# Moving a gate's sum to another stage, column groups for modulation sums, row halves for retention scores, and a shorter Newton step

## The chip, the cores and the metric

The kernel runs on one core of a Trainium2 chip. The metric is the device time of one execution of the program in microseconds (us). The engines are TensorE (PE), VectorE (DVE), ScalarE (ACT), GpSimd (POOL) and SyncE (SP); each runs its own list of instructions in order and waits on semaphores for the others. DMA transfers are issued from SP's, ACT's and POOL's lists.

## What is computed

One layer of a diffusion backbone over 1024 latent tokens (x) and 256 context tokens, 1024 wide, in fp32:

```python
mod = silu(c) @ w_ada + b_ada            # 1 x 6144
sh_a, sc_a, gt_a, sh_f, sc_f, gt_f = split(mod, 6)
h = rms_norm(x, g_attn) * (1 + sc_a) + sh_a      # context: the same with c_ctx
rq, rk, rv, rg, cq, ckv, kpe = split(h @ w_in)
y_ret = bidirectional chunkwise retention (4 heads, chunks of 128), group norm, swish gate
y_mla = multi-head latent attention (4 heads), keys from context and latent tokens
x_mid = x + gt_a * (concat(y_ret, y_mla) @ w_out)
h2 = rms_norm(x_mid, g_ffn) * (1 + sc_f) + sh_f
x = x_mid + gt_f * (square(relu(h2 @ w_ff1)) @ w_ff2)
out = rms_norm(x, g_final)
```

## The kernel before

Every product of fp32 operands is made as three matmuls on halves (`mm3`, L96 to L100): `split` (L102 to L104) makes a high half by an ACT cast and a low half by a DVE subtraction. The stages follow one another: modulations of the attention part, input projection, retention, attention, output projection, up stage and down stage of the MLP, final norm. A scheduler turns the program's order into one list for each engine. Large tiles live in 45 SBUF slots that are handed out first in, first out (`Slots`, L35 to L50), so a load can be issued when the slot's former user is done; small ones are in a ring of six (`tmp`); PSUM has eight banks, handed out in rings.

*Modulations.* gt_a, sh_f, sc_f and gt_f are the groups g=2, 3, 4 and 5 of 1024 columns of w_ada. For each, eight slices of w_ada (128 rows each, 512 KB) are loaded by SP (`mod_load`, L430; the load itself L160), and DVE adds them up, scaled by silu(c) of their row (`mod_step`, L435 to L450: L442 for the first, L444 for seven more). What is left is a sum over 128 partitions, made by PE with a matrix of ones (`mod_fin`, L455 to L473). Gates 2 and 5 are wanted as a row (L462): b_ada is added on one partition, the row goes to `g_dram`, and is loaded from there into all partitions. g=4 and g=3 are wanted as columns `mcol` (L471). The first modulations of the kernel, sh_a and sc_a, have their own code (L275 to L284): their matmuls with 32 columns of weights go to four 32-column groups, and a copy (L281) and transposes (L284) follow. g=2, 4 and 3 are summed in the input projection, g=5 in the output projection.

*Retention scores.* In `ret_a2` (L586 to L599) each chunk has four score matmuls (L597), two for each half of the 128 rows of `qkT`: heads g=0 on rows 0 to 63, g=1 on rows 64 to 127. Each half has its own bank, and two masks (`tt`) evacuate them.

*Newton step.* `rstd_of` (L106 to L119) makes 1/sqrt(v) by Ln and Exp on ACT and one Newton step on DVE, for each row of a tile. w is the number of values of a row; w=1 except for the group norm of retention.

*Output projection* (loop at L1323). 14 steps `wseq` over halves hf of the columns and token tiles t follow two that are issued earlier. At its start the four quarters of w_out's second half are loaded (L958), multiplied by gate gt_a (L959) and split. In the first eight steps two slices of g=5 are added and two loaded; the sum is finished at n == 9. `h2` is then normalised (L1354) and transposed (L245).

*Up stage* (loop over `order`, 112 steps). The product h2 @ w_ff1 is made by a Strassen-Winograd scheme: for each of 16 column pairs p there are seven products q of 12 matmuls. DVE and ACT prepare weights four steps ahead, evacuate the banks, and apply the squared ReLU; SP loads w_ff1 and stores the results (L1164).

Of the kernel before, what the change touches and what calls it, by code (L numbers as in the profile page):

```python
# [12 lines left out]
F32 = mybir.dt.float32  # L13
F32R = mybir.dt.float32r
AF = mybir.ActivationFunctionType
ALU = mybir.AluOpType
AX = mybir.AxisListType

P = 128
D = 1024  # L20
KD = D // P
# [7 lines left out]
EPS = 1e-6  # L29
# [24 lines left out]
def hymba_block(ctx: ExitStack, tc: tile.TileContext, A, K, out):  # L54
    nc = tc.nc
    V, S, T, G = nc.vector, nc.scalar, nc.tensor, nc.gpsimd
# [9 lines left out]
    psn = [0]  # L66
# [12 lines left out]
    def tmp(shape=(512,), dt=F32, half=False):  # L79
        n = math.prod(shape)  # L80
        if half:
            return tmpp.tile([P] + list(shape), dt, name="tmh", tag="tmh", bufs=TMH,
                             padded_shape=[P, 256] if len(shape) == 1 and n < 256 else None)
        return tmpp.tile([P] + list(shape), dt, name="tmp", tag="tmp",
                         padded_shape=[P, 512] if len(shape) == 1 and n < 512 else None)
# [7 lines left out]
    def tt(o, a, b, op):  # L93
        V.tensor_tensor(out=o, in0=a, in1=b, op=op)  # L94
# [10 lines left out]

    def rstd_of(ss, n, w, tag):  # L106
        v = sm(w, tag + "v")
        V.tensor_scalar(out=v, in0=ss, scalar1=1.0 / n, scalar2=EPS, op0=ALU.mult, op1=ALU.add)
        l = sm(w, tag + "l")
        S.activation(out=l, in_=v, func=AF.Ln)  # L110
        y = sm(w, tag + "y")
        S.activation(out=y, in_=l, func=AF.Exp, scale=-0.5)
        q = sm(w, tag + "q")
        tt(q, y, y, ALU.mult)
        tt(q, q, v, ALU.mult)
        V.tensor_scalar(out=q, in0=q, scalar1=-0.5, scalar2=1.5, op0=ALU.mult, op1=ALU.add)
        r = sm(w, tag + "r")
        tt(r, y, q, ALU.mult)
        return r  # L119

    x, ctxt = A["x"][0], A["ctx"][0]
# [308 lines left out]
    def mod_load(keep=1, last=24):  # L430
        if len(modq) > 32 - last and len(sl.free) > keep:
            g, kt = modq.pop(0)
            modr[g, kt] = load_wa(g, kt)
# [18 lines left out]
    bc = {}  # L452
    mcol = {}

    def mod_fin(g):  # L455
        m = mods[g]
        if g in (2, 5):
            row = sl.get((1024,))
            nc.gpsimd.dma_start(out=row[0][0:1, :], in_=A["b_ada"][:, g * 1024:(g + 1) * 1024])
            for j in range(2):  # L460
                ps = pT()
                T.matmul(ps, lhsT=ones, rhs=m[0][:, j * 512:(j + 1) * 512], start=True, stop=True)  # L462
                w = row[0][0:1, j * 512:(j + 1) * 512]
                tt(w, ps[0:1, :], w, ALU.add)
            nc.gpsimd.dma_start(out=g_dram[g // 4:g // 4 + 1, :], in_=row[0][0:1, :])
            sl.put(row)
        else:
            mcol[g] = const.tile([P, KD], F32, name=f"mcol{g}")
            ps = pT((KD, 64))
            for j in range(KD):  # L470
                T.matmul(ps[:, j, :], lhsT=m[0][:, j * P:(j + 1) * P], rhs=ones[:, 0:64], start=True, stop=True)  # L471
            tt(mcol[g], ps[:, :, 0], cols[:, b0 + g * 8:b0 + g * 8 + 8], ALU.add)
        sl.put(m)  # L473

    lg = const.tile([P, 8], F32, name="lg")
# [110 lines left out]
    def ret_a2(qkT, qw):  # L586
        ps = pT((4, P))
        for h in range(RH):
            T.transpose(ps[:, h, :], qw[:, h, :, :].rearrange("p a d -> p (a d)"), ident)
        qwT = tmp((4, P))  # L590
        S.copy(out=qwT, in_=ps)
        sT = tmp((2, 2, P))
        for g in range(2):
            ps = pT((2, P))
            o_ = 64 * g
            for i in range(2):
                T.matmul(ps[:, i, :], lhsT=qkT[o_:o_ + 64, 2 + i, :], rhs=qkT[o_:o_ + 64, i, :], start=True, stop=True)  # L597
            tt(sT[:, :, g, :], ps, dT.rearrange("p (i g) j -> p i g j", g=2)[:, :, g, :], ALU.mult)
        return sT, qwT  # L599

    def ret_b(n, o, sT, qwT):
# [535 lines left out]
    def bank(p, q):  # L1137
# [4 lines left out]
            pb[k] = psp.tile([P, 512], F32, name=f"ps{psn[0]}", tag=f"b{i}", bufs=1), i  # L1142
        return pb[k][0]

    def unbank(p, q):
        fbank.append(pb.pop((p, GRP[q]))[1])

# [174 lines left out]
    lag = Lag(1)  # L1322
    wseq = [(0, 2), (0, 3), (1, 0), (0, 4), (1, 1), (1, 2), (0, 5), (1, 3), (1, 4), (0, 6), (1, 5), (1, 6), (0, 7), (1, 7)]  # L1323
    for n, (hf, t) in enumerate(wseq):
        if n < 8:
            for _ in range(2):
                mod_step()
                mod_load(4, 32)
        if n < 2:
            load_wo(1, 2 * n)  # L1330
            load_wo(1, 2 * n + 1)
            wlag.flush()
        if n in (1, 4, 7, 10):
            load_y({1: 4, 4: 5, 7: 6, 10: 7}[n])
        if n == 2:
            sl.put(bc[2])
        wout_mm(hf, t, pG)
        if n == 9:
            while fins:
                mod_fin(fins.popleft())  # L1340
        if hf == 1:
            sl.put(*yt_[t])
            if t == 0:
                Af = const.tile([P, KD], F32, name="Af")
                V.scalar_tensor_tensor(out=Af, in0=mcol[4], scalar=1.0, in1=col("gf"), op0=ALU.add, op1=ALU.mult)
            if t % 4 == 0:
                for u in range(4):
                    h2r[u, t // 4] = sl.get((2, 512))
            sq = sl.get((1024,))
            ss = sm(1, "ss")  # L1350
            S.activation(out=sq[0], in_=acc[t][0], func=AF.Square, accum_out=ss)
            nc.gpsimd.dma_start(out=xm[t], in_=acc[t][0])
            r = rstd_of(ss, D, 1, "x")
            V.tensor_scalar(out=sq[0], in0=acc[t][0], scalar1=r, scalar2=None, op0=ALU.mult)  # L1354
            sl.put(acc[t])
            wt = slice((t % 4) * P, (t % 4 + 1) * P)
            lag.push(lambda t=t, sq=sq, wt=wt: h2_post(t, sq, wt))
        if (hf, t) == (1, 4):
            bsplit("B21", braw("B21"))
        if (hf, t) == (1, 5):  # L1360
            load_w1(0)
            bsplit("B11", braw("B11"))
        if (hf, t) == (0, 7):
            load_w1(1)
            for p, q in ((0, 2), (1, 2)):
                prep1(p, q)
# [26 lines left out]
    for s, (p, q) in enumerate(order):  # L1393
        w1_ahead(s)
        mm_1(p, q)
        post1(p, q)
        if s == 0:
            pairop(V, b11, b12, b11, ALU.subtract)
            bsplit("T1", b11)
        if s == 4:  # L1400
            pairop(V, b12, b22, b12, ALU.subtract)
            pairop(V, b11, b22, b11, ALU.subtract)
            bsplit("T2", b11)
        if s == 6:
            pairop(V, b21, b11, b21, ALU.subtract)
            sl.put(*b11)
            bsplit("T3", b12, True)
        if s == 9:
            bsplit("T4", b21, True)
        if s == 13:  # L1410
            bsplit("B22", b22, True)
        e = s - len(order)
        if e in (-10, -8, -6, -4):
            load2((10 + e) // 2)
        if e in (-5, -3):
            prep2((5 + e) // 2)
        print("S", e, s, p, q, len(sl.free), file=open("/tmp/sl.txt", "a"))
# [84 lines left out]
```

## Time and profile before

| | |
|---|---|
| three runs | 1288.75, 1289.8 and 1292.13 us; median 1289.8 |
| profiled execution | 1289.44 us |
| its span in the trace | 1287.7 us |
| busy: PE, DVE, ACT | 1254.3, 893.4, 653.7 us |

The span runs from the first to the last instruction that the trace holds; the other 1.74 us of the profiled execution lie around it. In the rows a bracket after an instruction gives how long its engine stood idle before it and what ended the idle time. The ends of matmuls are modelled, so from one matmul to the next the starts count. One matmul in the code can be two records (fp32 operands) in the profile; `x4` counts records. A name such as `u` stands for all slots.

### The profile page before, as it was taken

Reading aid. Unit: us, or ns where it says so; the run is one execution under the profiler, and the core shown is the slowest. Engines: PE = TensorE matmul, PEld = TensorE weight load, DVE = VectorE, ACT = ScalarE, POOL = GpSimd, SP = SyncE. Lnnn points to the kernel's source line nnn. Section 1 sums busy time; section 2 is a strip of 40 time slices with the busy share of each in tenths; the row PEclk is TensorE's granted clock in tenths of the full one; section 3 lists DMA queues with packets and bytes.
Section 4 is the critical chain, followed back from the end, with each engine's and each line's share of the span. In section 5 each row is a group of like instructions: output and inputs, shape, how many; then the busy total and the mean of one; then the engine's idle time right before and its main releaser. Section 6 shows DMA issues by size and latency. Waiting matters only on the chain.

```text
span 1287.7 us, 17814 instructions
## 1 busy us (share of the span) xinstructions
PE 1254.3 (97%) x6573; PEld 1059.7 (82%) x6573; DVE 893.4 (69%) x1799; ACT 653.7 (51%) x1361; POOL 16.8 (1%) x33
## 2 busy tenths in 40 slices
PE   5999999999999999999999999999999999999997
PEld 2688888999999998887878888888887888888885
DVE  3798676665687767986589766656668567676684
ACT  3761257754455556652457655555565434344441
POOL 0000000000000000000000000000000000000000
PEclk8999999999999999999999999999999999999999
DMA  9608401300001002544340454444579999986621
GB/s 343 234 29 281 149 30 45 111 14 1 1 10 37 10 25 68 187 132 155 115 148 33 169 174 155 163 140 148 180 244 340 407 412 353 350 292 239 237 102 78
DMA packets 95433, 204.13 MB, mean 159 GB/s; under 512 B 9193, under 2 KB 29362, under 8 KB 95346
## 3 DMA queue, kind: packets, MB, share of 16 engines
q1 hardware_dynamic: 92608, 194.55, 43.0%
q0 software_dynamic: 2480, 8.14, 1.7%
q8 instruction: 51, 0.84, 0.3%
q10 hardware_dynamic: 258, 0.30, 0.1%
q14 instruction: 36, 0.29, 0.1%
HBM read 152.89 MB, written 50.08 MB: 158 GB/s over the span
## 4 chain that ended last, share of the span: by engine, by line
PE 60%; issue 31%; DVE 3%; DMA 2%; ACT 2%; POOL 1%; SPq 0%; DVEq 0%; POOLq 0%; ACTq 0%
PE ps L100 19%; PE ps L98 19%; PE ps L99 19%; DVE u L104 1%; DMA udz<-u 1%; PE ps L301 1%; DVE u L519 1%; DVE u L94 1%; PE ps L513 1%; DMA u<-in_x_dram 0%; PE mps L275 0%; PE ps L604 0%; ACT u L103 0%; POOL y_dram L950 0%; DMA xm<-u 0%
## 5 line engine op out<-in xcount | busy, mean ns | idle before, releaser
L98 PE MATMUL ps<-u,u 128*128 128x512 f32 (+3 forms) x1664 | 618.2, 373 | 8.7 <-ACT u L322 4.3
L100 PE MATMUL ps<-u,u 128*128 128x512 f32 (+3 forms) x1664 | 612.9, 369 | 0.9 <-DVE u L94 0.6
L99 PE MATMUL ps<-u,u 128*128 128x512 f32 (+3 forms) x1664 | 613.4, 369 | 0.0
L98 PEld LDWEIGHTS ps<-u,u 128*128 128x128 f32 x1664 | 313.8, 189 | 63.5 <-ACT u L322 5.8
L100 PEld LDWEIGHTS ps<-u,u 128*128 128x128 f32 x1664 | 313.5, 188 | 52.9 <-DVE u L94 1.4
L99 PEld LDWEIGHTS ps<-u,u 128*128 128x128 f32 x1664 | 313.9, 189 | 48.7 <-issue 0.5
L104 DVE TENSOR_TENSOR u<-u,u 128x1024 fp32r<-128x1024 f32 (+4 forms) x247 | 250.9, 1034 | 112.8 <-ACT u L103 104.4
L103 ACT CAST u<-u 128x1024 fp32r<-128x1024 f32 (+3 forms) x247 | 217.5, 900 | 196.0 <-DVE u L94 58.3
L94 DVE TENSOR_TENSOR u<-ps,u 128x512 fp32r<-128x512 f32 (+3 forms) x218 | 134.8, 635 | 64.6 <-PE ps L100 48.0
L94 DVE TENSOR_TENSOR u<-u,u 128x512 f32<-128x512 f32 (+1 forms) x104 | 88.2, 852 | 38.0 <-ACT u L1161 18.0
L880 DVE TENSOR_REDUCE mx<-ps 128x1 f32<-128x512 f32 (+1 forms) x96 | 55.2, 597 | 25.7 <-PE ps L879 25.6
L1160 ACT ACTIVATE u<-u 128x512 f32<-128x512 f32 x64 | 40.3, 629 | 43.6 <-DVE u L94 43.5
L914 ACT CAST u<-ps 128x512 fp32r<-128x512 f32 (+1 forms) x96 | 45.1, 530 | 21.2 <-PE ps L912 21.2
L891 ACT ACTIVATE u<-ps,nm 128x512 f32<-128x512 f32 x64 | 43.6, 690 | 11.8 <-DVE nm L884 11.8
L444 DVE SCALAR_TENSOR_TENSOR u<-u,sc,u 128x1024 f32<-128x1024 f32 x28 | 35.8, 1281 | 9.2 <-DMA u<-in_w_ada_dram 8.7
L1161 ACT ACTIVATE u<-u 128x512 f32<-128x512 f32 x64 | 40.3, 631 | 1.5
L103 ACT CAST u<-tmp 128x512 fp32r<-128x512 f32 x32 | 19.7, 619 | 36.7 <-DVE u L94 27.3
L875 PE MATMUL ps<-u,u 128*128 128x512 f32 (+1 forms) x96 | 37.1, 387 | 0.6 <-ACT u L854 0.5
L912 PE MATMUL ps<-ident,u 128*128 128x128 f32 x256 | 35.1, 274 | 0.5 <-DVE nm L884 0.5
L878 PE MATMUL ps<-u,u 128*128 128x512 f32 (+1 forms) x96 | 34.6, 360 | 0.0
L877 PE MATMUL ps<-u,u 128*128 128x512 f32 (+1 forms) x96 | 34.4, 358 | 0.0
L876 PE MATMUL ps<-u,u 128*128 128x512 f32 (+1 forms) x96 | 34.1, 355 | 0.0
(207 smaller groups left out, 1107.6 us busy)
## 6 DMA issues: line engine op xcount, KB each, us to landing
u<-in_w_ff_dram SPq DMA_DIRECT2D x96, 512.0 KB, 6.3
u<-in_w_ada_dram SPq DMA_DIRECT2D x48, 512.0 KB, 4.8
u<-tdT SPq DMA_DIRECT2D x24, 512.0 KB, 10.1
u<-in_x_dram SPq DMA_DIRECT2D x16, 512.0 KB, 6.0
udy<-u SPq DMA_DIRECT2D x16, 512.0 KB, 4.0
udz<-u SPq DMA_DIRECT2D x16, 512.0 KB, 3.1
udw<-u SPq DMA_DIRECT2D x16, 512.0 KB, 4.6
u<-udy SPq DMA_DIRECT2D x16, 512.0 KB, 5.7
```

The lines of the kernel that those rows point to most:

```text
L94: V.tensor_tensor(out=o, in0=a, in1=b, op=op)
L98: T.matmul(ps, lhsT=lh, rhs=rh, start=start, stop=False, **kw)
L99: T.matmul(ps, lhsT=lh, rhs=rl, start=False, stop=False, **kw)
L100: T.matmul(ps, lhsT=ll, rhs=rh, start=False, stop=stop, **kw)
L103: S.copy(out=hi, in_=raw)
L104: (eng or V).tensor_tensor(out=lo, in0=raw, in1=f(hi), op=ALU.subtract)
L875: T.matmul(ps[:, 0:n], lhsT=qh, rhs=kh, start=True, stop=False)
L880: V.reduce_max(out=mx[:, kb:kb + 1], in_=ps[:, 0:n], axis=AX.X)
L891: S.activation(out=dst[kb], in_=ps[:, 0:n], func=AF.Exp, scale=SCALE, bias=nm, accum_out=su[:, kb:kb + 1])
L914: S.copy(out=hi, in_=ps[:, 0:m, :])
L1160: S.activation(out=ap, in_=ap, func=AF.Relu)
L1161: S.activation(out=ap, in_=ap, func=AF.Square)
```

## The change

`rstd_of` keeps v as -4 times its value, so that the Newton step is two operations at w=1 (three else). `mod_fin` makes all four sums in four column groups of 256 columns into one bank; for g=2 and 5 the row then lies on four partitions, with b_ada loaded and the result stored in quarters by POOL; for g=4 and 3 a copy by ACT and two transposes make the columns. `ret_a2` takes both banks first and issues the scores with alternating halves. g=5's slices are loaded and added in the up stage, one for each of the pairs 4 to 12 behind product q=5, and finished in pair 13; a bank for it comes from the up stage's own queue.

```diff
--- before.py
+++ after.py
@@ -105,17 +105,19 @@
 
     def rstd_of(ss, n, w, tag):
         v = sm(w, tag + "v")
-        V.tensor_scalar(out=v, in0=ss, scalar1=1.0 / n, scalar2=EPS, op0=ALU.mult, op1=ALU.add)
+        V.tensor_scalar(out=v, in0=ss, scalar1=-4.0 / n, scalar2=-4.0 * EPS, op0=ALU.mult, op1=ALU.add)
         l = sm(w, tag + "l")
-        S.activation(out=l, in_=v, func=AF.Ln)
+        S.activation(out=l, in_=v, func=AF.Ln, scale=-1.0)
         y = sm(w, tag + "y")
         S.activation(out=y, in_=l, func=AF.Exp, scale=-0.5)
         q = sm(w, tag + "q")
-        tt(q, y, y, ALU.mult)
-        tt(q, q, v, ALU.mult)
-        V.tensor_scalar(out=q, in0=q, scalar1=-0.5, scalar2=1.5, op0=ALU.mult, op1=ALU.add)
+        if w == 1:
+            V.scalar_tensor_tensor(out=q, in0=y, scalar=v, in1=y, op0=ALU.mult, op1=ALU.mult)
+        else:
+            tt(q, y, y, ALU.mult)
+            tt(q, q, v, ALU.mult)
         r = sm(w, tag + "r")
-        tt(r, y, q, ALU.mult)
+        V.scalar_tensor_tensor(out=r, in0=q, scalar=3.0, in1=y, op0=ALU.add, op1=ALU.mult)
         return r
 
     x, ctxt = A["x"][0], A["ctx"][0]
@@ -452,24 +454,28 @@
     bc = {}
     mcol = {}
 
-    def mod_fin(g):
+    def mod_fin(g, ring=None):
         m = mods[g]
+        ps = (ring or pT)()
+        for j in range(4):
+            T.matmul(ps[32 * j:32 * j + 32, 0:256], lhsT=ones[:, 0:32], rhs=m[0][:, j * 256:(j + 1) * 256], start=True, stop=True)
         if g in (2, 5):
-            row = sl.get((1024,))
-            nc.gpsimd.dma_start(out=row[0][0:1, :], in_=A["b_ada"][:, g * 1024:(g + 1) * 1024])
-            for j in range(2):
-                ps = pT()
-                T.matmul(ps, lhsT=ones, rhs=m[0][:, j * 512:(j + 1) * 512], start=True, stop=True)
-                w = row[0][0:1, j * 512:(j + 1) * 512]
-                tt(w, ps[0:1, :], w, ALU.add)
-            nc.gpsimd.dma_start(out=g_dram[g // 4:g // 4 + 1, :], in_=row[0][0:1, :])
-            sl.put(row)
+            row = tmp((256,))
+            V.memset(row, 0.0)
+            for j in range(4):
+                nc.gpsimd.dma_start(out=row[32 * j:32 * j + 1, :], in_=A["b_ada"][:, g * 1024 + j * 256:g * 1024 + (j + 1) * 256])
+            tt(row, ps[:, 0:256], row, ALU.add)
+            for j in range(4):
+                nc.gpsimd.dma_start(out=g_dram[g // 4:g // 4 + 1, j * 256:(j + 1) * 256], in_=row[32 * j:32 * j + 1, :])
         else:
             mcol[g] = const.tile([P, KD], F32, name=f"mcol{g}")
-            ps = pT((KD, 64))
-            for j in range(KD):
-                T.matmul(ps[:, j, :], lhsT=m[0][:, j * P:(j + 1) * P], rhs=ones[:, 0:64], start=True, stop=True)
-            tt(mcol[g], ps[:, :, 0], cols[:, b0 + g * 8:b0 + g * 8 + 8], ALU.add)
+            ms = tmp((256,))
+            S.copy(out=ms, in_=ps[:, 0:256])
+            ps = (ring or pT)((2, P))
+            for i in range(2):
+                T.transpose(ps[:, i, :], ms[:, i * P:(i + 1) * P], ident)
+            tt(mcol[g].rearrange("p (j i) -> p j i", i=2), ps.rearrange("p i (j r) -> p j i r", r=32)[:, :, :, 0],
+               cols[:, b0 + g * 8:b0 + g * 8 + 8].rearrange("p (j i) -> p j i", i=2), ALU.add)
         sl.put(m)
 
     lg = const.tile([P, 8], F32, name="lg")
@@ -590,12 +596,13 @@
         qwT = tmp((4, P))
         S.copy(out=qwT, in_=ps)
         sT = tmp((2, 2, P))
+        pss = [pT((2, P)) for _ in range(2)]
+        for i in range(2):
+            for g in range(2):
+                o_ = 64 * g
+                T.matmul(pss[g][:, i, :], lhsT=qkT[o_:o_ + 64, 2 + i, :], rhs=qkT[o_:o_ + 64, i, :], start=True, stop=True)
         for g in range(2):
-            ps = pT((2, P))
-            o_ = 64 * g
-            for i in range(2):
-                T.matmul(ps[:, i, :], lhsT=qkT[o_:o_ + 64, 2 + i, :], rhs=qkT[o_:o_ + 64, i, :], start=True, stop=True)
-            tt(sT[:, :, g, :], ps, dT.rearrange("p (i g) j -> p i g j", g=2)[:, :, g, :], ALU.mult)
+            tt(sT[:, :, g, :], pss[g], dT.rearrange("p (i g) j -> p i g j", g=2)[:, :, g, :], ALU.mult)
         return sT, qwT
 
     def ret_b(n, o, sT, qwT):
@@ -1142,6 +1149,12 @@
             pb[k] = psp.tile([P, 512], F32, name=f"ps{psn[0]}", tag=f"b{i}", bufs=1), i
         return pb[k][0]
 
+    def fring():
+        i = fbank.popleft()
+        fbank.append(i)
+        psn[0] += 1
+        return psp.tile([P, 512], F32, name=f"ps{psn[0]}", tag=f"b{i}", bufs=1)
+
     def unbank(p, q):
         fbank.append(pb.pop((p, GRP[q]))[1])
 
@@ -1322,10 +1335,6 @@
     lag = Lag(1)
     wseq = [(0, 2), (0, 3), (1, 0), (0, 4), (1, 1), (1, 2), (0, 5), (1, 3), (1, 4), (0, 6), (1, 5), (1, 6), (0, 7), (1, 7)]
     for n, (hf, t) in enumerate(wseq):
-        if n < 8:
-            for _ in range(2):
-                mod_step()
-                mod_load(4, 32)
         if n < 2:
             load_wo(1, 2 * n)
             load_wo(1, 2 * n + 1)
@@ -1335,9 +1344,6 @@
         if n == 2:
             sl.put(bc[2])
         wout_mm(hf, t, pG)
-        if n == 9:
-            while fins:
-                mod_fin(fins.popleft())
         if hf == 1:
             sl.put(*yt_[t])
             if t == 0:
@@ -1409,6 +1415,11 @@
             bsplit("T4", b21, True)
         if s == 13:
             bsplit("B22", b22, True)
+        if q == 5 and 4 <= p <= 12:
+            mod_step()
+            mod_load(2, 32)
+        if q == 5 and p == 13:
+            mod_fin(fins.popleft(), fring)
         e = s - len(order)
         if e in (-10, -8, -6, -4):
             load2((10 + e) // 2)
```

### The order at three places

In the rows, L and a number is the line in that kernel's own file, then the operation, output and inputs, and the shape. `u` tiles are slots in SBUF, `ps` tiles PSUM banks, `tmp` small buffers.

VectorE at the start of the output projection, before (L444 is the sum over g=5, L959 the gate folded into a w_out quarter, L104 the low half of a split, L94 with `ps` an evacuation):

```order
L444 SCALAR_TENSOR_TENSOR u_6642<-u_6644,sc,u_6642 128x1024
L94 TENSOR_TENSOR u_5990<-ps_6480,u_5990 128x512
L94 TENSOR_TENSOR u_6457<-ps_6506,u_6456 128x4x128
L94 TENSOR_TENSOR u_6459<-ps_6513,u_6458 128x4x128
L94 TENSOR_TENSOR u_6460<-ps_6520,u_6460 128x2x128
L959 TENSOR_TENSOR u_6646<-u_6646,u_5631 128x1024
L959 TENSOR_TENSOR u_6649<-u_6649,u_5631 128x1024
L104 TENSOR_TENSOR u_6653<-u_6646,u_6652 128x1024
L104 TENSOR_TENSOR u_6657<-u_6649,u_6656 128x1024
L959 TENSOR_TENSOR u_6695<-u_6695,u_5631 128x1024
L444 SCALAR_TENSOR_TENSOR u_6642<-u_6687,sc,u_6642 128x1024
L94 TENSOR_TENSOR u_6058<-ps_6558,u_6058 128x512
```

The same place now (L966 is the gate folding, the old L959):

```order
L966 TENSOR_TENSOR u_6597<-u_6597,u_5588 128x1024
L94 TENSOR_TENSOR u_5947<-ps_6437,u_5947 128x512
L966 TENSOR_TENSOR u_6600<-u_6600,u_5588 128x1024
L94 TENSOR_TENSOR u_6414<-ps_6463,u_6413 128x4x128
L94 TENSOR_TENSOR u_6416<-ps_6470,u_6415 128x4x128
L94 TENSOR_TENSOR u_6417<-ps_6477,u_6417 128x2x128
L104 TENSOR_TENSOR u_6604<-u_6597,u_6603 128x1024
L104 TENSOR_TENSOR u_6608<-u_6600,u_6607 128x1024
L966 TENSOR_TENSOR u_6637<-u_6637,u_5588 128x1024
L966 TENSOR_TENSOR u_6640<-u_6640,u_5588 128x1024
L104 TENSOR_TENSOR u_6644<-u_6637,u_6643 128x1024
L94 TENSOR_TENSOR u_6015<-ps_6515,u_6015 128x512
```

The operations of g=5 are gone from between; the first gate multiply now stands ahead of the first evacuation, and the evacuation of the next product (u_6015, before u_6058) stands behind all four gate multiplies and three of their splits.

The SP queue at the same place, before (L160 is a slice of w_ada, L958 a quarter of w_out, L980 a tile of x, L975 one of y):

```order
L160 DMA u_6744<-in_w_ada_dram 128x1024
L160 DMA u_6640<-in_w_ada_dram 128x1024
L160 DMA u_6644<-in_w_ada_dram 128x1024
L958 DMA u_6646<-in_w_out_dram 128x2x512
L958 DMA u_6649<-in_w_out_dram 128x2x512
L958 DMA u_6695<-in_w_out_dram 128x2x512
L160 DMA u_6687<-in_w_ada_dram 128x1024
L160 DMA u_6690<-in_w_ada_dram 128x1024
L958 DMA u_6692<-in_w_out_dram 128x2x512
```

and now (L965 is the load of w_out):

```order
L965 DMA u_6189<-in_w_out_dram 128x2x512
L965 DMA u_6282<-in_w_out_dram 128x2x512
L965 DMA u_6597<-in_w_out_dram 128x2x512
L965 DMA u_6600<-in_w_out_dram 128x2x512
L965 DMA u_6637<-in_w_out_dram 128x2x512
L965 DMA u_6640<-in_w_out_dram 128x2x512
L987 DMA u_6657<-in_x_dram 128x1024
L987 DMA u_6764<-in_x_dram 128x1024
```

The four loads of w_out's second half (from u_6597 on) follow one another, with no slice of w_ada between or ahead of them.

TensorE at the scores of chunk 1, before (L597; L589 are transposes of the weighted queries):

```order
L100 MATMUL ps_1677<-u_1501,u_279 128x512
L597 MATMUL ps_1620<-tmp 128x128 x2
L589 MATMUL ps_1612<-ident,tmp 128x128 x4
L597 MATMUL ps_1624<-tmp 128x128 x2
L604 MATMUL ps_1628<-u_1104,tmp 128x128
```

and now (L603, L595):

```order
L603 MATMUL ps_1620<-tmp 128x128
L603 MATMUL ps_1621<-tmp 128x128
L595 MATMUL ps_1612<-ident,tmp 128x128 x4
L603 MATMUL ps_1620<-tmp 128x128
L603 MATMUL ps_1621<-tmp 128x128
L611 MATMUL ps_1628<-u_1096,tmp 128x128
```

Two matmuls into one bank become one into each of two banks, at the same two places around the transposes.

## Rows read from the trace of the kernel before

**Rows 1.** The page: part 1 (busy us, share, instructions) and part 4 (the chain):

```profile
PE 1254.3 (97%) x6573; PEld 1059.7 (82%) x6573; DVE 893.4 (69%) x1799; ACT 653.7 (51%) x1361; POOL 16.8 (1%) x33
...
PE 60%; issue 31%; DVE 3%; DMA 2%; ACT 2%; POOL 1%; SPq 0%; DVEq 0%; POOLq 0%; ACTq 0%
```

**Rows 2.** PE's timeline at two sums (start, length, operation, count, idle before):

```profile
112.68 1.88 PE L462 MATMUL ps<-u,ones 128*128 128x512 f32 x4
114.00 0.79 PE L98 MATMUL ps<-u,u 128*128 128x512 f32 x1
...
133.47 1.90 PE L471 MATMUL ps<-ones,u 128*128 128x64 f32 x16
```

**Rows 3.** PE's timeline early on: two transposes, and matmuls in column groups:

```profile
20.14 0.44 PE L284 MATMUL ps<-ident,tmp 128*128 128x128 f32 x2 [0.50 <-ACT tmp L281]
...
35.98 1.07 PE L275 MATMUL mps<-u,u 128*32 128x256 f32 x16
37.10 0.50 PE L98 MATMUL ps<-u,u 128*128 128x512 f32 x1
```

**Rows 4.** PE's timeline, retention scores of three chunks:

```profile
174.04 0.71 PE L597 MATMUL ps<-tmp 64*128 64x128 f32 x4
...
179.72 0.48 PE L597 MATMUL ps<-tmp 64*128 64x128 f32 x2
...
190.79 0.72 PE L597 MATMUL ps<-tmp 64*128 64x128 f32 x8
```

**Rows 5.** Timelines of DVE and PE, first Newton step; DVE's last one:

```profile
14.49 0.15 DVE L116 TENSOR_SCALAR xq<-xq 128x1 f32<-128x1 f32 x1
14.68 0.16 DVE L94 TENSOR_TENSOR xr<-xy,xq 128x1 f32<-128x1 f32 x1
...
15.68 0.47 PE L301 MATMUL ps<-ident,u 128*128 128x128 f32 x1 [0.95 <-DVE u L236]
...
1282.24 0.16 DVE L94 TENSOR_TENSOR xr<-xy,xq 128x1 f32<-128x1 f32 x1
```

**Rows 6.** DVE's timeline, start of the output projection:

```profile
567.12 1.28 DVE L444 SCALAR_TENSOR_TENSOR u<-u,sc,u 128x1024 f32<-128x1024 f32 x1 [1.79 <-DMA u<-in_w_ada_dram]
...
575.14 1.22 DVE L959 TENSOR_TENSOR u<-u,u 128x1024 f32<-128x1024 f32 x1
578.78 1.29 DVE L444 SCALAR_TENSOR_TENSOR u<-u,sc,u 128x1024 f32<-128x1024 f32 x1 [2.42 <-DMA u<-in_w_ada_dram]
579.98 0.69 DVE L94 TENSOR_TENSOR u<-ps,u 128x512 f32<-128x512 f32 x1
```

**Rows 7.** PE's timeline, its waits in the output projection:

```profile
569.66 0.39 PE L98 MATMUL ps<-u,u 128*128 128x256 f32 x1 [0.93 <-DVE u L94]
...
580.72 0.50 PE L98 MATMUL ps<-u,u 128*128 128x512 f32 x1 [2.18 <-DVE u L94]
...
652.12 1.06 PE L245 MATMUL ps<-ident,u 128*128 128x128 f32 x8 [0.90 <-DVE u L1354]
```

**Rows 8.** SP's timeline, one load of w_out; landing of all L958's loads:

```profile
571.27 0.37 SPq L958 DMA_DIRECT2D u<-in_w_out_dram  x1
...
DMA to landing us min/median/max: 4.4/6.6/8.4
```

**Rows 9.** DVE's timeline before PE's wait at 652.12:

```profile
643.07 0.67 DVE L94 TENSOR_TENSOR u<-ps,u 1x512 f32<-1x512 f32 x1
...
645.69 1.23 DVE L104 TENSOR_TENSOR u<-u,u 128x1024 fp32r<-128x1024 f32 x1 [0.82 <-DMA g_dram<-u]
```

**Rows 10.** Up stage by windows: length, busy by engine, clock, DMA share, GB/s:

```profile
790.00:810.00 20.00, 20.00 (x90) 16.44 (x89) 13.11 (x22) 10.52 (x18) 0.00 (x0) 1.00 0.44 146
```

**Rows 11.** Up stage: SP's and DVE's timelines; landing of all L160's loads:

```profile
781.29 0.52 SPq L1164 DMA_DIRECT2D udy<-u  x1
...
788.96 0.69 DVE L94 TENSOR_TENSOR u<-u,u 128x512 f32<-128x512 f32 x1 [1.36 <-ACT u L1161]
...
DMA to landing us min/median/max: 3.2/4.6/7.8
```

## The prediction

> **What bounds the kernel now.** I read the page's busy times first and then its chain. TensorE (PE) is busy 1254.3 of 1287.7 us, and the chain that ended last is PE for 60% and PE without any visible wait ("issue") for 31% [rows 1]. So only three kinds of microsecond count: one that PE works less, one that PE waits less, and one at the two ends of the program, where PE has nothing to do. I then read PE's timeline at the modulation sums [rows 2], at work that already runs in column groups [rows 3] and at the retention scores [rows 4]; the two ends [rows 5]; the idle times of VectorE (DVE) and PE at the start of the output projection [rows 6, 7], with the SP queue behind them [rows 8]; a wait late in that stage [rows 7, 9]; and last the up stage, into which work moves [rows 10, 11].
>
> **The change, part by part.** The profiled execution took 1289.44 us, 0.36 below the median of the three runs (1289.8). The sum is made against 1289.44.
>
> *Sums of g=2 and g=5.* Each is now two matmuls with a full block of ones: from 112.68 to the next product at 114.00, which itself comes into rhythm 0.4 late (0.79 long where 0.39 is usual) [rows 2], 1.72 in all. The new form is four matmuls of 256 columns in four 32-column groups. The start of the kernel has that form: 16 records, which are eight such matmuls, go from 35.98 to 37.10, and the product behind is 0.1 late [rows 3], so 1.2. Four matmuls take at least half of that, 0.6, and as entering and leaving the block does not halve, I take 0.85. Saving 0.87 each, **1.74** for both. g=5's new place costs the 0.85 in the up stage instead, where PE is full too; that is in the number. At most, if the groups cost nothing, 3.4; at least 0, if they ran one after another, since 4 x 256 columns are 2 x 512.
>
> *Sums of g=4 and g=3.* Now 16 records of 64 columns, as long in the profile as the pair (1.90 beside 1.88 [rows 2]), so I take 1.75. New: 0.85 for the groups and two transposes, which took 0.44 with their modelled end where the trace has two [rows 3]; I take 0.3. Saving 0.6 each, **1.2** for both; 1.5 at most, and nothing if the groups do not overlap. The transposes wait for an ACT copy; PE has products between, so I count no wait.
>
> *Retention scores.* The diff alternates the two row halves so that they run side by side. The trace shows that they already do: four matmuls (eight records) took 0.72, but two on one half (four records) also 0.71, and one (two records) 0.48 [rows 4]. Where all four stand together, in six of eight chunks, the order inside the block is worth nothing. In chunk 1 the two halves are torn apart by transposes, two blocks of 0.71; there the new order makes two of one pair, about 0.48 each. Gain 2 x 0.23 = **0.46**. In chunk 2 the order stays. Bounds: 0, and half of a 0.72 block in six chunks more, 2.2. The Trainium skill ("TensorEngine Tiling (Array Packing)", key properties and gotcha 1) has row tiles run independently but not on one PSUM bank at a time, up to twice as fast; its rule would count the halving in every chunk. By it the sum would be 2.2 lower; [rows 4] speak against it, as the two banks already overlap.
>
> *Newton step.* At w=1 four small DVE operations become two; they stand 0.19 apart [rows 5]. That is on the path at the start, where PE waits 0.95 for the scaled row at 15.68, and at the very end, where the same chain stands before the last scaling at 1282.24 [rows 5]. 2 x 0.39 = **0.78** (0.39 if the first wait is taken over by a weight slice). In between it is hidden by PE's work, with one exception below.
>
> *The moved step.* Eight multiply-adds of g=5, 1.28 each [rows 6], and eight 512 KB loads leave the output projection. It is not their work that costs there but where they wait: DVE stood 1.79 for a w_ada slice before 567.12 and 2.42 before 578.78 [rows 6]. Behind the first stand evacuations that PE waited 0.93 for; behind the second, the evacuation at 579.98 that gives back the bank PE waited 2.18 for [rows 6, 7]. What is late next? The w_out loads, which now follow one another on SP. The one issued at 571.27 had landed when DVE used it at 575.14, so within 3.9 [rows 6, 8]; its slot is freed by the last attention products, so the last of the four will be issued near 571 again. With that landing the chain is load 575, gate multiply 1.2, split 1.2, evacuation 0.6: 578.2, against PE's arrival at 580.72 - 2.18 = 578.5, less what PE gains just before, about 1.1 (0.6 of the 0.93, and two matmuls that now come later). So about 0.8 of the 2.18 stays, and 0.3 of the 0.93, in all **-2.0**. Bounds: -3.1 if both go; with the median landing of 6.6 the evacuation ends near 581 and the gain is about 0; with the longest, 8.4 [rows 8], it is a loss of 2. I take the first since fewer loads share the queue.
>
> *The later wait.* PE waits 0.90 for the scaled row before the transposes at 652.12 [rows 7]. DVE loses in front of it the two one-row adds of g=5's end (0.6 each), a 0.82 wait for their store to free a slot [rows 9], and 0.39 of Newton step: 2.4. PE, without the two ones-matmuls just before (1.72), arrives 1.72 earlier, so 2.62 would be needed to clear the wait: 0.2 stays, **-0.7**. Bounds -0.9 and, if DVE does not move, +1.7.
>
> *Up stage.* The eight adds come to 10.3 us of DVE over 8 column pairs of 19 us; DVE is busy 13.1 of 20 there and PE 20.00 of 20.00 [rows 10]. The load stands on SP behind the store at 781.29, which takes 0.52; with the median landing of 4.6 it is there at 786.4, with the longest, 7.8, at 789.6 [rows 11]. On DVE the add stands just ahead of the subtraction at 788.96, before which DVE idles 1.36 for ACT [rows 11]: the add fits that gap. Cost 0; 1.9 per pair on DVE if every load takes the longest. DMA carries 146 GB/s there, and one load in 19 us adds 27. The b_ada quarters and row stores sit on POOL, which has nothing else due; their memset comes long before the sums.
>
> **Sum.** -1.74 - 1.2 - 0.46 - 0.78 - 2.0 - 0.7 = -6.9: **1282.5**; against the median instead, 1282.9.
>
> **Rivals.**
> - *The output projection keeps its wait*: the last w_out load lands as the median one did, and DVE holds the bank as long as now. For it: that load cannot be issued before its slot is free. Against: [rows 6]. The 2.0 goes: **1284.5**.
> - *The halves gain in every chunk*: a block of four falls from 0.72 to half of it in the six chunks left as they are, 2.2 more: **1280.3**. Against it [rows 4]. This is what the rule cited above would make of it.
> - *The groups run one after another*: no gain from the sums, 2.9 back: **1285.4**. Against: [rows 3].
> - *PE catches up with DVE and loads*: three of the four sums lie where DVE was itself busy with w_ada slices; a faster PE meets operands that were just in time, and the 2.1 of those three sums (0.87 + 1.2) is given back, with the 2.0 of the output projection: **1286.6**, no change. For it: the waits of [rows 7] show how near DVE runs.
> - *Slower*: in the up stage every add blocks DVE until its slice lands, 789.6 + 1.2 in place of 788.96, 1.9 late for eight pairs, and PE waits the whole of it for its evacuations or weight splits: 8 x 1.9 = 15, **1297.7**. It decides from 0.9 per pair (6.9 / 8), and is measurably slower from 1.35 (another 3.9 / 8). For it: the add is in DVE's order, and SP issues the load only behind a store. Against: DVE's 6.9 spare in 20 us, and four steps of preparation ahead.
>
> **How the numbers follow.** Forecast 0.50; output projection unchanged 0.20; halves 0.05; groups in turn 0.05; caught up 0.13; slower 0.07. A measurement of this kernel tells 0.3%, 3.9 us, from no change, so faster means below 1285.9. The first four cases lie there with 0.80, of which I put 0.03 over the edge, since 1284.5 and 1285.4 are near it: 0.77 faster; 0.16 within; 0.07 slower. Range 1278.8 (halves, and the two waits gone whole) to 1286.8 (caught up), which leaves the slower case, about half of the caught-up one and a little below it outside.
>
> **What would show it.** Right: sums of 0.85 where 1.72 stood; a score block of four still 0.7 long; DVE with no wait for w_ada near 567 and 579 and PE's wait before the third output product under 1 us; the start shorter by 0.4; no PE waits in the up stage. Wrong: score blocks near 0.4; a DVE wait for w_out of 3 us at the start of the output projection; PE waits repeating every 19 us in the up stage beside DVE waits for w_ada.

## The result, and the profile after

The changed kernel took 1279.22 us in the median of four runs (1278.58 to 1280.07), the kernel before 1289.47 (four runs). The ratio is 0.992, with a 95% interval of 0.9907 to 0.9932: 10.25 us less, where 6.9 were forecast. The time lies in the range; the direction was right, and the size fell a third short.

The page of the kernel after, part 1 and part 4 (beside [rows 1]):

```profile
PE 1250.3 (98%) x6569; PEld 1055.0 (83%) x6569; DVE 882.6 (69%) x1715; ACT 656.6 (51%) x1363; POOL 22.9 (2%) x45
...
PE 58%; issue 34%; DMA 4%; DVE 2%; POOL 1%; ACT 1%; SPq 0%; DVEq 0%; POOLq 0%; ACTq 0%
```

PE works 4.0 us less. The rest is waiting, and the end of the program. PE's list of waits after (line, released by what: us in all, times, longest):

```profile
PE mps L277 <- DMA u<-in_w_ada_dram: 8.3, 5, 5.4
...
PE ps L98 <- DVE u L94: 1.2, 2, 1.0
...
PE ps L631 <- DVE u L94: 0.8, 1, 0.8
PE ps L303 <- DVE u L238: 0.8, 2, 0.7
```

The waits of 0.93, 2.18 and 0.90 [rows 7] are not in it. Of the two that make L98's 1.2, one is what is left of the 2.18 (0.19, below), and the other, 1.04 at 962.08, had been 1.09 before. The 8.3 us at the top are the start's first weights, and L631's 0.8 is a wait that was 0.5 before.

PE's timeline at two sums (g=2 and g=4), which answer to [rows 2]:

```profile
111.48 0.64 PE L461 MATMUL ps<-u,ones 128*32 128x256 f32 x8
112.05 0.50 PE L98 MATMUL ps<-u,u 128*128 128x512 f32 x1
...
131.34 0.64 PE L461 MATMUL ps<-u,ones 128*32 128x256 f32 x8
131.91 0.50 PE L98 MATMUL ps<-u,u 128*128 128x512 f32 x1
...
132.72 0.38 PE L476 MATMUL ps<-ident,tmp 128*128 128x128 f32 x2
132.86 0.47 PE L98 MATMUL ps<-u,u 128*128 128x512 f32 x1
```

and the product behind the sum of g=4 in the kernel before:

```profile
135.18 0.48 PE L98 MATMUL ps<-u,u 128*128 128x512 f32 x1
```

The block is 0.57 from start to start, and the product behind it is 0.50 long instead of 0.39, so 0.68 in all. Before, g=2 took 1.72 and g=4, reckoned the same way from 133.47, 1.80 (the prediction took 1.75). The two transposes at 132.72 cost about 0.2. PE's timeline at the scores of chunk 1, which answer to [rows 4]:

```profile
171.04 0.49 PE L603 MATMUL ps<-tmp 64*128 64x128 f32 x4
...
172.04 0.49 PE L603 MATMUL ps<-tmp 64*128 64x128 f32 x4
...
187.32 0.71 PE L603 MATMUL ps<-tmp 64*128 64x128 f32 x8
```

Both torn blocks hold one matmul on each half and take 0.49, as forecast; a whole block of eight records is as long as before. At the two ends, PE's first wait for the scaled row, and DVE's last Newton step (beside [rows 5]):

```profile
14.82 0.90 PE L303 MATMUL ps<-ident,u 128*128 128x128 f32 x3 [0.66 <-DVE u L238]
```

```profile
1271.96 0.22 DVE L115 SCALAR_TENSOR_TENSOR xq<-xy,xv 128x1 f32<-128x1 f32 x1 [0.50 <-ACT xy L112]
1272.22 0.16 DVE L120 SCALAR_TENSOR_TENSOR xr<-xq,xy 128x1 f32<-128x1 f32 x1
```

At the start of the output projection, DVE's timeline after (beside [rows 6]):

```profile
566.94 1.22 DVE L966 TENSOR_TENSOR u<-u,u 128x1024 f32<-128x1024 f32 x1
569.39 1.22 DVE L966 TENSOR_TENSOR u<-u,u 128x1024 f32<-128x1024 f32 x1 [1.23 <-DMA u<-in_w_out_dram]
570.53 1.22 DVE L104 TENSOR_TENSOR u<-u,u 128x1024 fp32r<-128x1024 f32 x1
571.67 0.68 DVE L94 TENSOR_TENSOR u<-ps,u 128x512 f32<-128x512 f32 x1
```

PE's only wait there ([rows 7] had two):

```profile
572.41 0.50 PE L98 MATMUL ps<-u,u 128*128 128x512 f32 x1 [0.19 <-DVE u L94]
```

and the landing times of all w_out loads, min, median and max (beside [rows 8]):

```profile
DMA to landing us min/median/max: 3.5/4.2/4.6
```

DVE stands once for a load, 1.23 for w_out at 569.39, and the evacuation at 571.67 gives the bank back in time for a wait of 0.19. The loads land in 4.2 in the median, where it was 6.6. In the up stage PE waits 0.21 for the first weights, at 660.09, and then no more until the 1.04 at 962.08. SP's timeline of one pair, and DVE's, with the landing times of the slices there:

```profile
770.09 0.52 SPq L1177 DMA_DIRECT2D udy<-u  x1
773.48 0.34 SPq L162 DMA_DIRECT2D u<-in_w_ada_dram  x1
```

```profile
777.60 1.28 DVE L446 SCALAR_TENSOR_TENSOR u<-u,sc,u 128x1024 f32<-128x1024 f32 x1
```

```profile
DMA to landing us min/median/max: 3.3/3.3/3.3
```

The slice is issued at 773.48, lands 3.3 later at 776.8, and is added at 777.60. It is there with 0.8 us to spare.

### The profile page after: what moved, and what is told of

Its sections match the earlier page's. It is cut to its first block, busy times and chain, and to the rows that moved or that the text cites. A ratio compares the mean times of both kernels' runs of the same rounds, so it can differ in the third digit from the quotient of the medians.

```text
span 1277.1 us, 17776 instructions
## 1 busy us (share of the span) xinstructions
PE 1250.3 (98%) x6569; PEld 1055.0 (83%) x6569; DVE 882.6 (69%) x1715; ACT 656.6 (51%) x1363; POOL 22.9 (2%) x45
## 4 chain that ended last, share of the span: by engine, by line
PE 58%; issue 34%; DMA 4%; DVE 2%; POOL 1%; ACT 1%; SPq 0%; DVEq 0%; POOLq 0%; ACTq 0%
PE ps L98 18%; PE ps L100 18%; PE ps L99 18%; DMA u<-in_x_dram 2%; DMA u<-in_w_ada_dram 1%; DVE u L525 1%; PE ps L519 1%; DMA xm<-u 0%; DVE u L104 0%; PE ps L303 0%; POOL y_dram L957 0%; DMA u<-in_w_ff_dram 0%; PE ps L611 0%; POOL y_dram L635 0%; DVE u L94 0%
## 5 line engine op out<-in xcount | busy, mean ns | idle before, releaser
L98 PE MATMUL ps<-u,u 128*128 128x512 f32 (+3 forms) x1664 | 617.4, 372 | 5.5 <-ACT u L324 4.0
L98 PEld LDWEIGHTS ps<-u,u 128*128 128x128 f32 x1664 | 313.8, 189 | 61.2 <-ACT u L324 5.5
L104 DVE TENSOR_TENSOR u<-u,u 128x1024 fp32r<-128x1024 f32 (+4 forms) x247 | 250.2, 1031 | 104.0 <-ACT u L103 94.8
L94 DVE TENSOR_TENSOR u<-ps,u 128x512 fp32r<-128x512 f32 (+3 forms) x214 | 132.1, 632 | 74.5 <-PE ps L100 53.0
L94 DVE TENSOR_TENSOR u<-u,u 128x512 f32<-128x512 f32 (+1 forms) x104 | 88.0, 850 | 28.1 <-ACT u L622 8.5
L446 DVE SCALAR_TENSOR_TENSOR u<-u,sc,u 128x1024 f32<-128x1024 f32 x28 | 35.8, 1281 | 4.8 <-DMA u<-in_w_ada_dram 4.2
L882 PE MATMUL ps<-u,u 128*128 128x512 f32 (+1 forms) x96 | 37.1, 387 | 0.6 <-ACT u L861 0.4
L885 PE MATMUL ps<-u,u 128*128 128x512 f32 (+1 forms) x96 | 34.6, 360 | 0.0
L884 PE MATMUL ps<-u,u 128*128 128x512 f32 (+1 forms) x96 | 34.4, 358 | 0.0
L883 PE MATMUL ps<-u,u 128*128 128x512 f32 (+1 forms) x96 | 34.1, 355 | 0.0
L886 PE MATMUL ps<-u,u 128*128 128x512 f32 (+1 forms) x96 | 34.1, 355 | 0.0
```

Source lines behind the costliest of these rows:

```text
L98: T.matmul(ps, lhsT=lh, rhs=rh, start=start, stop=False, **kw)
L104: (eng or V).tensor_tensor(out=lo, in0=raw, in1=f(hi), op=ALU.subtract)
L882: T.matmul(ps[:, 0:n], lhsT=qh, rhs=kh, start=True, stop=False)
```

## The experiments

The theory on trial (A) is the prediction's sum: each part has a price where PE works less or waits less, and the moved step's price is DVE's standing among the w_out quarters. Against it stand the rivals: small operations that hold up DVE everywhere, halves that ran in turn, a saving that PE gives back in waits, an output projection that keeps its wait, and DVE blocked in the up stage.

**Four parts, each alone on the kernel before.** e1 takes the new `rstd_of`, e2 the new `mod_fin`, e3 the new score order, e4 the moved step with the old sum:

```diff
 e1:
...
-        tt(q, y, y, ALU.mult)
...
+            V.scalar_tensor_tensor(out=q, in0=y, scalar=v, in1=y, op0=ALU.mult, op1=ALU.mult)
...
 e2:
...
-                T.matmul(ps, lhsT=ones, rhs=m[0][:, j * 512:(j + 1) * 512], start=True, stop=True)
...
+            T.matmul(ps[32 * j:32 * j + 32, 0:256], lhsT=ones[:, 0:32], rhs=m[0][:, j * 256:(j + 1) * 256], start=True, stop=True)
...
 e3:
...
-            for i in range(2):
...
+        for i in range(2):
+            for g in range(2):
...
 e4:
...
-        if n < 8:
-            for _ in range(2):
-                mod_step()
-                mod_load(4, 32)
...
+        if q == 5 and 4 <= p <= 12:
+            mod_step()
+            mod_load(2, 32)
```

> The kernel before with the shorter Newton step alone. Theory A (the parts add up, and this one counts only where PE waits for it): PE's first wait for the scaled row falls from 0.95 to about 0.6, the tail is 0.4 shorter, the wait of 0.90 before the transposes at 652.12 falls by 0.4: 1.0 to 1.2 us faster than before, no more. Theory B (the small operations hold up DVE at every tile): over 2 us faster, with PE waits gone elsewhere too.

> The kernel before with the four modulation sums in column groups alone. Theory A: each block of ones-matmuls falls from 1.7 to 0.65, less 0.2 for two transposes at g=4 and g=3, so 3.5 to 4 us of PE work less; g=5's end no longer has its two one-row adds, but the out-projection's waits of 0.93 and 2.18 stay: 3.5 to 4.5 us faster. Theory B (PE catches up with operands that are just in time): the sums before the retention are given back in waits, 1 to 2 us faster.

> The kernel before with the alternating score order alone. Theory A (the two halves ran side by side already): the two torn blocks of chunk 1 fall from 0.71 to 0.49, all other blocks keep their length; 0.4 us faster, which is within the noise. Theory B (each chunk's block is halved): 2 to 2.6 us faster, blocks of eight records near 0.4.

> The kernel before with g=5's loads, adds and end moved to the up stage alone (its sum still two matmuls of 512 columns). Theory A (it is DVE's stand for w_ada slices, and with them the w_out loads in the queue, that PE waits for): PE's waits of 0.93 and 2.18 nearly vanish and so does the one at 652.12 in part; the sum costs in the up stage what it saves in the output projection: 3.5 to 4.5 us faster. Theory B (the output projection's start is bound by the slots that w_out waits for): 1 us or less faster, and the wait for the third product's bank stays near 2 us.

Against 1290.31 us of the kernel before on the same chip: e1 1288.15 (ratio 0.998, 0.9971 to 0.9988), e2 1285.2 (0.9959, 0.9947 to 0.9971), e3 1289.02 (0.9991, 0.9981 to 1.0), e4 1285.68 (0.9963, 0.9952 to 0.9975). e2 and e4 are the change: 5.1 and 4.6 us. With e2 at 5.1 (3.7 to 6.8 by its interval), PE does not give the sums back in waits. e1's 2.2 is more than A gave it, and its profile says why: neither the wait of 0.93 nor that of 0.90 is in it. But neither wait is the Newton step's alone: in e2 the 0.93 is 1.1 and the 0.90 is gone, and in e3, which touches neither place, the 0.93 is gone too and the 0.90 is 1.4. The kernel before stood 1.79 for a slice of w_ada ahead of the 0.93 [rows 6]; in e3 the same add starts without a wait:

```profile
564.44 1.28 DVE L444 SCALAR_TENSOR_TENSOR u<-u,sc,u 128x1024 f32<-128x1024 f32 x1
```

There is one trace of each kernel, so how often the kernel before has this wait is not known. The four savings add to 13.2 us, and the whole change saves 9 to 10. The 0.93 is missing in e1, e3 and e4 and the 0.90 in e1, e2 and e4, so about 3 us of the sum are counted more than once; what is left is within the intervals. The wait for the third product's bank is another matter. It is there in e1, DVE first and PE behind:

```profile
578.27 1.28 DVE L446 SCALAR_TENSOR_TENSOR u<-u,sc,u 128x1024 f32<-128x1024 f32 x1 [3.08 <-DMA u<-in_w_ada_dram]
```

```profile
580.21 0.50 PE L98 MATMUL ps<-u,u 128*128 128x512 f32 x1 [2.61 <-DVE u L94]
```

and in e4 nearly gone, with no w_ada wait ahead of it but one for w_out:

```profile
574.46 1.23 DVE L959 TENSOR_TENSOR u<-u,u 128x1024 f32<-128x1024 f32 x1 [1.26 <-DMA u<-in_w_out_dram]
```

```profile
577.47 0.50 PE L98 MATMUL ps<-u,u 128*128 128x512 f32 x1 [0.21 <-DVE u L94]
```

**The change without the move** (e5: g=5's steps and its end put back into the output projection).

```diff
+        if n < 8:
+            for _ in range(2):
+                mod_step()
+                mod_load(4, 32)
...
-        if q == 5 and 4 <= p <= 12:
-            mod_step()
-            mod_load(2, 32)
```

> The changed kernel with g=5's loads, adds and end put back into the output projection, at the places they had before. Theory A (the move takes PE's waits away, and nothing else of the change does): the wait for the bank of the third product is back at 2 to 2.6 us beside DVE waits for w_ada of over 2 us; 4 to 5 us slower than the changed kernel, so 5 to 6.5 us faster than before. Theory B (the lighter DVE of the other parts would have cleared these waits too): within 2 us of the changed kernel.

1285.01 us, ratio 0.9963 (0.9949 to 0.9977). That is 4.5 below the kernel before on its chip, a little less than the 5 to 6.5 expected, and by the ratios 4.5 to 5.5 above the changed kernel. PE's two waits are back, with a DVE wait for w_out ahead of the first and one for w_ada ahead of the second:

```profile
566.48 0.39 PE L98 MATMUL ps<-u,u 128*128 128x256 f32 x1 [0.96 <-DVE u L94]
...
577.49 0.74 PE L98 MATMUL ps<-u,u 128*128 128x512 f32 x1 [2.14 <-DVE u L94]
```

```profile
564.60 1.23 DVE L966 TENSOR_TENSOR u<-u,u 128x1024 f32<-128x1024 f32 x1 [1.27 <-DMA u<-in_w_out_dram]
...
575.55 1.28 DVE L446 SCALAR_TENSOR_TENSOR u<-u,sc,u 128x1024 f32<-128x1024 f32 x1 [2.46 <-DMA u<-in_w_ada_dram]
```

The wait for the third product's bank goes with the move and with no other part: it is 2.1 to 2.6 in e1, e2, e3 and e5. The same can't be said of the 0.96, which e1 and e3 lack without the move.

**The same work, later in the stage** (e6, on the kernel before).

```diff
-        if n < 8:
+        if 3 <= n < 11:
...
-        if n == 9:
+        if n == 12:
```

> The kernel before, with g=5's steps still in the output projection but at its steps n=3 to 10 instead of 0 to 7, and the end at n=12. DVE has the same 10 us of adds in the stage; only they and their loads no longer stand among the w_out quarters. Theory A (what costs is where DVE stands and waits, not the work): PE's wait of 2.18 falls under 1 us, 1.5 to 3 us faster than before. Theory B (the adds' work holds the bank back): no change.

1287.05 us, ratio 0.9981 (0.9972 to 0.9991). The waits of 0.93 and 2.18 are both gone, although DVE does the same ten microseconds of adds in the stage, and the w_out loads land in 3.7 in the middle, with one slice of w_ada just ahead of them instead of three:

```profile
DMA to landing us min/median/max: 3.6/3.7/5.3
```

So it is not the adds' work that costs in this stage, but their place. A new wait appears where the up stage's first weights are split (PE's list of waits, and ACT's timeline just before it):

```profile
PE ps L98 <- ACT u L103: 3.0, 1, 3.0
```

```profile
668.44 0.62 ACT L103 CAST u<-u 128x512 fp32r<-128x512 f32 x1 [1.61 <-DMA u<-in_w_ff_dram]
```

It gives a good part back. ACT stood 1.61 for a load of w_ff1 there; that the later end of g=5 held this load up is not shown.

**The transfers without the adds** (e10: eight slices loaded in the output projection, nobody reads them; on the changed kernel).

```diff
+        if n < 4:
+            for j in range(2):
+                if len(sl.free) > 4:
+                    sl.put(load_wa(5, 2 * n + j))
```

> The changed kernel itself once more, beside the two that follow. All theories: 9 to 11 us faster than before; PE's waits in the output projection under 0.3 us.

> The changed kernel with eight loads of w_ada slices put back between the w_out loads on SP, into slots that are free and with nobody who reads them: the transfers of before without the adds that waited for them. Theory A (the w_out quarters land late because the queue is shared, and DVE stands for them in the adds' stead): landing of w_out back at 6 us in the middle, DVE waits of 2 us or more for w_out, PE's wait for the third product's bank 1.5 to 2.5 us; 2 to 4 us slower than the changed kernel. Theory B (what held the bank was DVE standing in the adds): DVE waits under 1.5 us, PE's wait under 0.7, within 1.5 us of the changed kernel.

Beside each other on one chip: the changed kernel 1280.12 (ratio 0.9928, 0.9914 to 0.9943), e10 1281.68 (0.9946, 0.9932 to 0.996). The intervals overlap, so the 1.6 us are not certain. What is plain is the landing of w_out in e10, and DVE's stand for it:

```profile
DMA to landing us min/median/max: 5.2/6.2/8.9
```

```profile
573.96 0.69 DVE L94 TENSOR_TENSOR u<-ps,u 128x512 f32<-128x512 f32 x1 [3.14 <-PE ps L100]
577.46 1.23 DVE L966 TENSOR_TENSOR u<-u,u 128x1024 f32<-128x1024 f32 x1 [2.81 <-DMA u<-in_w_out_dram]
```

The middle is back at 6.2, from 3.6 in the changed kernel's run beside it: the eight loads alone make w_out late. They do so in two ways, as the last two quarters are also issued later, at 570.0 and 570.5 instead of 563.7 and 567.1. And one of PE's two waits is back, at the place of the 0.93, with no add anywhere near (DVE first, then PE):

```profile
564.53 1.23 DVE L966 TENSOR_TENSOR u<-u,u 128x1024 f32<-128x1024 f32 x1 [1.18 <-DMA u<-in_w_out_dram]
```

```profile
566.41 0.39 PE L98 MATMUL ps<-u,u 128*128 128x256 f32 x1 [1.08 <-DVE u L94]
```

The wait for the third product's bank did not come back, but not because of B: the scheduler put its evacuation, at 573.96, ahead of that gate multiply here. How much of 2.18 each of the two, the shared queue and the standing adds, would cost by itself in the old order stays open.

**Both row halves on one** (e8, on the kernel before).

```diff
-            o_ = 64 * g
+            o_ = 0
```

> The kernel before with all four score matmuls of a chunk on the same row half, rows 0 to 63 (heads of g=1 get g=0's scores, so part of the scores is left out). Theory A (on two halves they ran side by side): blocks of eight records rise from 0.72 to 1.1 to 1.2, six or seven chunks by 0.45: 2.5 to 3.5 us more PE time. Theory B (they ran one after another in this order): blocks keep 0.72, no change.

1291.52 us, ratio 1.0018 (1.0008 to 1.0028): 2.0 us slower, 1.0 to 3.6 by the interval. PE's timeline, a torn block of chunk 1 and the first whole block:

```profile
173.41 0.71 PE L597 MATMUL ps<-tmp 64*128 64x128 f32 x4
...
190.13 1.16 PE L597 MATMUL ps<-tmp 64*128 64x128 f32 x8
```

The whole block of eight records takes 1.16 where [rows 4] have 0.72, and the torn one keeps 0.71; six whole blocks come to 2.6 us. The halves overlapped all along, in the old order, and the alternating order has nothing left to gain in a whole block.

**The slower rival, made to happen.** e7 adds four and e11 two further DVE operations of 1.28 us on the slice behind each add of the up stage (seven, since the first slice is only multiplied); e12 is e11 with each slice loaded one step of the sum earlier (the diff shows e7; in e11 and e12 the count is 2).

```diff
+            if g == 5:
+                for _ in range(4):
+                    V.scalar_tensor_tensor(out=r[0], in0=r[0], scalar=sc[:, kt:kt + 1], in1=r[0],
+                                           op0=ALU.mult, op1=ALU.add)
 e12 also:
-            mod_step()
+            if p > 4:
+                mod_step()
             mod_load(2, 32)
+            if p == 4:
+                mod_load(2, 32)
```

> The changed kernel with four further operations of 128x1024 on the slice after each of the eight adds of g=5 in the up stage (5.1 us of DVE more per pair; they write a slice that nobody reads any more). It is the slower rival's price measured. Theory A (DVE has 5 to 6 us to spare per pair, and weights are prepared four steps ahead): at most 1 us of PE waits in all, within 2 us of the changed kernel. Theory B (evacuations or splits behind the adds are what PE waits for): 1 to 5 us of PE wait per pair, 10 to 40 us slower.

> As the kernel with four further operations behind each of g=5's adds in the up stage, with two (2.6 us of DVE more per pair). Theory A (PE waits once DVE's spare time of a pair is used up, at about 5 us): no PE waits in the up stage, as the changed kernel. Theory B (each us behind the adds reaches PE): 0.6 to 0.8 us of wait per pair, half of what four cost, 5 us slower.

> The changed kernel with two further operations behind each add, as before, but with every slice of g=5 loaded one step of the sum earlier, so that two are under way. Theory A (what PE waited for with the further operations was DVE standing for the slice, 1.8 us a pair, not the work): no DVE waits for w_ada in the up stage, PE waits there under 1 us in all, within 2 us of the changed kernel. Theory B (the work of 2.6 us a pair is what reaches PE): PE waits of 5 to 7 us in all stay, near 1287 to 1289.

e7: 1290.01 us (ratio 1.0003, 0.9993 to 1.0013). e11: 1288.64 (0.9998, 0.999 to 1.0007). e12: 1282.03 (0.9947, 0.9934 to 0.9961). Four operations cost 10.8 us against 1279.22, and two cost 8.5 beside the changed kernel's 1280.12: almost the same, so it is not their work, and both theories had the wrong cause for e7 and e11. PE's waits in the two (e7 first):

```profile
PE ps L98 <- ACT u L1202: 8.0, 6, 2.0
```

```profile
PE ps L98 <- ACT u L1202: 6.3, 6, 1.4
```

The timelines of e11: SP's, with the landing times of the slices, then DVE's, ACT's and PE's:

```profile
775.05 0.52 SPq L1181 DMA_DIRECT2D udy<-u  x1
775.66 0.56 SPq L162 DMA_DIRECT2D u<-in_w_ada_dram  x1
...
DMA to landing us min/median/max: 5.0/5.0/5.0
```

```profile
781.39 1.28 DVE L446 SCALAR_TENSOR_TENSOR u<-u,sc,u 128x1024 f32<-128x1024 f32 x1 [1.77 <-DMA u<-in_w_ada_dram]
```

```profile
784.56 0.62 ACT L103 CAST u<-u 128x512 fp32r<-128x512 f32 x1 [2.94 <-DVE u L94]
785.08 0.58 ACT L1202 COPY u<-ps 128x512 f32<-128x512 f32 x1
```

```profile
785.72 0.50 PE L98 MATMUL ps<-u,u 128*128 128x512 f32 x1 [1.14 <-ACT u L1202]
```

DVE stands 1.77 for the slice in front of the add, with its evacuations and splits behind it; ACT stands 2.94 for one of these operations, and the copy that PE waits for follows on ACT. It is the rival's mechanism, though PE waits six times and not eight, and for less than DVE does. What the further operations changed is when the slice lands: 5.0 after its issue, against 3.3. SP issues it 0.61 behind a store, where the changed kernel has 3.39 between the two (770.09 and 773.48); that the store beside it makes it slow is likely, but no run shows it by itself. In e12 DVE is as busy and the slice is early. The stretch from 780 to 875 in the two (length, then busy PE, PEld, DVE, ACT, POOL, clock, DMA share, GB/s), e11 and then e12:

```profile
780.00:875.00 95.00, 89.65 (x391) 72.59 (x390) 74.00 (x105) 48.26 (x82) 0.00 (x0) 1.00 0.52 168
```

```profile
780.00:875.00 95.00, 95.00 (x419) 77.95 (x418) 76.90 (x108) 52.49 (x90) 0.00 (x0) 1.00 0.54 182
```

DVE does 76.9 us of work in 95 in e12 and PE is never idle; in e11 it does less, 74.0, and PE loses 5.35. Here waiting in order costs, and the same work without the wait costs PE nothing in this stretch. e12 as a whole is not quite the changed kernel: by the ratios it stays 2.4 to 3.5 us above it. PE has one wait of 0.90 in its up stage, at 765.08, outside this stretch; the rest is not explained.

## Why the prediction was right, and where it fell short

- *Sums.* Right in kind, too small. Forecast 0.85 for a block; it takes 0.68. With the ones-matmuls' 1.72 that is 2.1 for g=2 and g=5 instead of 1.74, and about 1.8 for the other two instead of 1.2 (1.80 less 0.68 and two transposes of about 0.2). e2, which has them alone, gained 5.1, more than the sums' 4; the 0.90, missing from its trace, is the likely rest. The step that failed is "entering and leaving the block does not halve": the block of four matmuls was nearly half of the block of eight.
- *Scores.* Right: 0.71 to 0.49 twice, nothing elsewhere. The gain from overlap had been had before: e8 shows 1.16 without it and 0.72 with it, in the old order. The Trainium skill ("TensorEngine Tiling (Array Packing)", overview and key properties) has row tiles execute in parallel, up to twice as fast. The runs agree that they run side by side, and not with the reading that they must alternate to do so.
- *Newton step.* Right in place, a little too large. The start's wait fell from 0.95 [rows 5] to 0.66 and the tail has two operations less, but behind the first of those left the next starts 0.26 later, where 0.19 was usual: about 0.3 at each end, not 0.39. The first product came 1.09 earlier in this trace, but 0.58 of that is a weight slice that landed sooner (PE's matmul at 13.65 began at 13.07), which the change does not touch. e1's 2.2 holds both small waits besides.
- *The moved step.* Right in cause (e4, e5, e6), too small: 0.93 and 2.18 became 0.19, 2.9 instead of 2.0. The term that was off is PE's remaining wait of 0.8 plus 0.3. The last w_out load was taken to be used at 575.14; in e4, where PE reaches this place at nearly the forecast time (577.26 without its wait, forecast 577.4), SP issued it at 570.80, 0.5 earlier than the 571.27 of [rows 8], and DVE used it at 574.46, 3.7 later. As to the 0.93, e1 and e3 lack it without the move, so only the 2.18 is shown to be the move's.
- *The later wait.* 0.90 went whole, 0.7 forecast. But e1, e2 and e5 lose it without the move, and in e3 it grows to 1.4 with nothing near it changed, so the term was less certain than its bounds, and that the move takes it is not shown.
- *Up stage.* Right that it costs nothing, by 0.8 us. The adds come to 9.7 us and not 10.3, as the first is a multiply of 0.74. The prediction's margin (the gap of 1.36 ahead of the subtraction) was reckoned for DVE's work; what decided was whether the slice lands before the add. The chance of 0.07 was on the right mechanism, and e11 gives its price: 8.5 us, 6.3 of it in six listed waits, not 15.
- *Not in the sum.* A wait of 0.53 in the attention that is absent after, the sooner slice at the start, and 0.3 more at L631. Such waits come and go in e1 to e4 too.
- *The range.* That the time lies in it is in part luck. Its lower end, 1278.8 (1279.0 by the terms named for it), took in 2.2 for score halves that gain in every chunk, which the blocks of 0.71 rule out. Without them it would end near 1281, above both 1279.22 and the second run's 1280.12.

## What to carry to other kernels

An in-order engine with time to spare is not free to take work: what counts is whether its operand has landed when its turn comes, so load a step earlier before moving work onto it. A block's price is best read from the same block at another size elsewhere in the trace, and what two sizes cost tells entry and size apart. Before counting a gain from overlap, look whether blocks of one and of two already take the same time; and savings of waits under 1 us do not add up, since several edits remove the same wait, and some come and go between kernels that do not touch them.

## What the runs showed that I had not expected

Two row halves run side by side when two matmuls on one are followed by two on the other: 0.72 for all four, 0.71 for the two of one half, 1.16 for four on one half. And eight unread loads of 512 KB raised the median landing of the w_out quarters from 3.6 to 6.2 us, and brought a wait of 1.08 of PE back.
